# A two-block diffusion transformer on one core: the first layer's shift and scale as TensorE products in four column groups

## The chip, the cores and the metric

The kernel runs on one NeuronCore of a Trainium2 chip. The metric is the device time of one execution in microseconds (us); the reported number is the median of several executions. Lower is better. The engines that appear below are TensorE (PE in the profile; its weight loads are PEld), VectorE (DVE), ScalarE (ACT), GpSimd (POOL) and SyncE (SP), whose queue issues all loads and stores.

## The reference

256 tokens of 1024 features pass through four transformer layers, two of a first block and two of a second. Everything is float32. Each layer makes six modulation vectors of 1024 numbers from a condition vector `c`, and uses two of them, a shift and a scale, before its mixer:

```python
c_act = jax.nn.silu(c)
mod = jnp.einsum('bd,dm->bm', c_act, w_mod[i]) + b_mod[i]     # 1024 -> 6 * 1024
sh_a, sc_a, gt_a, sh_f, sc_f, gt_f = jnp.split(mod, N_MOD, axis=-1)
h = modulate(rmsnorm(x, g_mix_pre[i]), sh_a, sc_a)            # norm * (1 + scale) + shift
qkv = jnp.einsum('bsd,de->bse', h, w_qkv[i])
```

After `qkv` come a stick-breaking attention, an output projection and a gated feed-forward network; the other three layers are alike in form. All that matters here is the very beginning: layer 0 can't start its first projection before the shift and scale of its features exist, and these are 2 x 1024 dot products of length 1024 against 8.4 MB of weights.

## The kernel before, in words

**Precision.** Weights arrive in float32. Most products are made three times in a reduced format (`mm3`, line 611): each operand is split into a rounded part (`wh`, `hh`) on ACT and a remainder (`wl`, `hl`) on DVE (`split`, line 601), and the products high-high, high-low and low-high are added in PSUM.

**Loads.** Weights come as 1 MB chunks (`chunk`, line 594; 128 partitions x 2048 floats) through SP's queue. A chunk needs one of 3 buffers of class K8; a half chunk (128 x 1024 floats) needs one of 32 buffers of class K4.

**Order.** The builder records every operation in program order. A planner (`schedule`, line 382) then replays them with a cost for each operation and picks, whenever an engine is free, the ready operation that was recorded first; the result is a fixed order per engine for the whole program. At run time each engine follows its order strictly. All operations are issued from one helper, so the profile's line is always L543 and tiles have to be told apart by name.

**The first stage** (`first_values`, line 966) makes layer 0's values `v` (256 x 1024). It runs over four rounds `q`, each with two of the eight feature tiles of 128. `mods(q)` loads four half chunks of modulation weights and makes the shift and the scale for the two tiles; then the transposed, normalized tokens (`tps`) are scaled and shifted to `hf` and split to `h0h`/`h0l` (tiles 0 to 3) or `h1h`/`h1l` (4 to 7); then the round's 1 MB chunk of value weights is split and 24 products of 128 x 512 are added into the PSUM tiles `acc`. In the recorded order `mods(q + 1)` stands ahead of the 24 products of round `q`. When `acc` is complete, ACT copies it out as `v` and the query and key projections (`qkps`) begin.

In the kernel before, `mods` makes each column by a dot product on DVE: the weights are laid out transposed, so that partition p holds the 1024 weights of output feature p, and `dot` (line 673) multiplies them with `c_act`, which TensorE has spread over all partitions (`on_all_rows`, the tiles `rowps` and `rows`), and adds along the row. The bias enters as the starting value. There are 16 such dot products in the stage (2 vectors x 8 tiles); `scale_of` (line 684) then turns a scale into (1 + scale) * gain.

Of the kernel before, what the change touches and what calls it, by code (L numbers as in the profile page):

```python
# [10 lines left out]
F32 = mybir.dt.float32  # L11
# [3 lines left out]
ALU = mybir.AluOpType  # L15
AX = mybir.AxisListType
PSUM = bass.MemoryType.PSUM

P = 128
D = 1024  # L20
S = 256
KT = D // P
# [559 lines left out]
class Builder:  # L582
# [41 lines left out]
    def setup(self):  # L624

        nc, io = self.nc, self.io
        self.mhalf = self.const.tile([P, 16], F32, tag="mhalf", name="mhalf")
        nc.gpsimd.memset(self.mhalf, -0.5)
        self.cact = self.const.tile([P, 24], F32, tag="cact", name="cact")
        nc.sync.dma_start(out=self.cact, in_=self.io["vecs"][:, 0:24])  # L630
        self.eye = self.const.tile([P, P], F32, tag="eye", name="eye")
        nc.sync.dma_start(out=self.eye, in_=io["consts"][:, 0:P])
        self.vec = self.const.tile([P, NVEC], F32, tag="vec", name="vec")
        nc.sync.dma_start(out=self.vec[:, 0 : self.FIRST], in_=self.io["vecs"][:, 0 : self.FIRST])
        nc.scalar.activation(out=self.cact, in_=self.cact, func=AF.Silu)
        self.cb = {0: self.on_all_rows(self.cact[:, 0:8])}

    def setup_x(self):
# [327 lines left out]
    def first_values(self):  # L966

        nc, io = self.nc, self.io
        self.setup()
        acc = self.new_acc()  # L970
        self.h = self.new_ht("h")
        self.raw["sc_a"] = self.sb.tile([P, 8], F32, name="raw")

        def mods(q):
            for k in range(2):
                f = q * 2 + k
                i = len(self.plan)
                self.plan.append([("w_mod", 0, None, 1, a * D + f * P, D) for a in range(2)])
                for a, kind in enumerate(("sh_a", "sc_a")):
                    w = self.sb.tile([P, D], F32, name="w0")  # L980
                    nc.sync.dma_start(out=w, in_=io["wst"][i][:, a * D : (a + 1) * D])
                    if f + a == 0:
                        self.setup_x()
                    self.dot(w, self.cb[0], 0, 0, kind, f)
                self.scale_of(0, 0, "sc_a", f, 1)

        mods(0)
        xn = [self.normed(self.x[t], None, self.xe[t]) for t in range(2)]
        for q in range(4):
            w = self.w.load()  # L990
            tps = self.first_tps(xn, q)
            for k in range(2):
                kt = q * 2 + k
                a, b = self.modcols["sc_a"][:, kt : kt + 1], self.modcols["sh_a"][:, kt : kt + 1]
                h = self.sb.tile([P, 2, P], F32, name="hf")
                if k == 0:
                    nc.vector.tensor_scalar(out=h, in0=tps[:, k], scalar1=a, scalar2=b, op0=ALU.mult, op1=ALU.add)
                else:
                    nc.scalar.activation(out=h, in_=tps[:, k], func=AF.Identity, scale=a, bias=b)
                hh, hl = self.hm(self.h, kt)  # L1000
                nc.scalar.copy(hh, h)
                nc.vector.tensor_tensor(out=hl, in0=h, in1=hh.bitcast(F32), op=ALU.subtract)
            if q < 3:
                mods(q + 1)
            w = self.w.take(w)
            for t in range(2):
                for k in range(2):
                    self.acc_mm(acc, t, self.hx(self.h, t, q * 2 + k), w[k], q + k == 0, q + k == 4)
        nc.after = nc.ops[-1]
        self.setup_rest()  # L1010
        nc.after = None
        return self.evict_v(acc)
# [629 lines left out]
```

## Time and profile before

| | |
|---|---|
| median of 3 runs | 1364.46 us (1360.81 to 1364.98) |
| the profiled execution's own time | 1364.06 us |
| span of that execution's instructions | 1362.2 us |
| mean granted TensorE clock | 0.991 of full speed |
| HBM read | 309.35 MB |

All stretches below are microseconds from the start of the span. A "busy" share of PE counts the modelled length of pipelined products, so a PE that is busy 10 of 10 us may still work more slowly than it can; the spacing of the starts of its products says more. DVE, ACT and DMA shares can be read as they stand. A bracket behind a row of the timeline gives the idle time of that engine before the instruction and what ended it. A merged row (x4) gives the start of its first instruction.

### The profile page before, as it was taken

The numbers are of one execution on the slowest core, as the hardware profiler recorded it, in microseconds if no ns is written. First come the engines' busy times: TensorE is split into PE (matmuls) and PEld (weight loads), VectorE is DVE, ScalarE is ACT, GpSimd is POOL, SyncE is SP. The second block draws the span as 40 slices with busy tenths as digits, with TensorE's granted clock in tenths as the row PEclk, the third lists the DMA queues.
The fourth block names the chain that finished last, engine by engine and source line by source line (L and its number), as shares of the span: only waits on it lengthen the run. The fifth ranks groups of instructions, "written<-read, shape, count | busy, mean of one in ns | idle before, by whom it ended". The sixth has DMA issues, their size and how long they took to land.

```text
span 1362.2 us, 22161 instructions
## 1 busy us (share of the span) xinstructions
PE 1327.6 (97%) x8872; PEld 1195.2 (88%) x8872; DVE 1084.7 (80%) x1817; ACT 715.6 (53%) x1241; POOL 73.0 (5%) x102
## 2 busy tenths in 40 slices
PE   5999899999999999999999999999999999899998
PEld 4887799999888799999888888899999899899997
DVE  7888888998988599999799987876767998755542
ACT  3664665555666474546543567854444536544430
POOL 0000100000100000001023111200000000000000
PEclk8999899999999999999999999999999999999999
DMA  9856578887676156777454531587776688455520
GB/s 361 322 223 255 207 280 318 321 327 294 240 250 263 50 201 255 278 257 281 182 187 158 212 121 66 190 315 255 273 277 255 228 311 307 147 194 186 186 94 32
DMA packets 45319, 311.83 MB, mean 229 GB/s; under 512 B 5280, under 2 KB 5664, under 8 KB 8864
## 3 DMA queue, kind: packets, MB, share of 16 engines
q1 hardware_dynamic: 45216, 310.42, 61.2%
q8 instruction: 69, 1.13, 0.3%
q14 instruction: 34, 0.28, 0.1%
HBM read 309.35 MB, written 1.05 MB: 228 GB/s over the span
## 4 chain that ended last, share of the span: by engine, by line
PE 92%; DVE 4%; ACT 2%; issue 1%; DMA 0%; POOL 0%; SPq 0%; ACTq 0%; DVEq 0%
PE gu L543 34%; PE acc L543 31%; PE qkps L543 7%; PE fp L543 4%; PE cu L543 3%; PE z L543 2%; PE dz L543 2%; PE bb L543 2%; PE qps L543 2%; DVE w L543 1%; PE op L543 1%; PE dop L543 1%; PE kc L543 1%; PE tps L543 1%; PE atp L543 1%; DVE u L543 1%
## 5 line engine op out<-in xcount | busy, mean ns | idle before, releaser
L543 DVE TENSOR_TENSOR wl<-w,wh 128x1024 fp32r<-128x1024 f32 x392 | 471.3, 1221 | 77.3 <-ACT wh L543 54.3
L543 ACT CAST wh<-w 128x1024 fp32r<-128x1024 f32 x392 | 402.8, 1049 | 102.9 <-DMA w<-in_wst_dram 62.2
L543 DVE CUSTOM_DVE_ANT_0 w<-w,rows,vec 128x1024 f32<-128x1024 f32 x192 | 242.2, 1279 | 12.9 <-DMA w<-in_wst_dram 12.7
L543 PE MATMUL gu<-h1h,wh 128*128 128x256 f32 x640 | 181.4, 283 | 0.0
L543 PE MATMUL gu<-h1h,wl 128*128 128x256 f32 x640 | 181.1, 283 | 0.0
L543 PE MATMUL gu<-h0h,wl 128*128 128x256 f32 x640 | 181.1, 283 | 0.0
L543 PE MATMUL gu<-h1l,wh 128*128 128x256 f32 x640 | 181.1, 283 | 0.0
L543 PE MATMUL gu<-h0l,wh 128*128 128x256 f32 x640 | 181.1, 283 | 0.0
L543 PE MATMUL gu<-h0h,wh 128*128 128x256 f32 x640 | 181.0, 283 | 0.0
L543 PE MATMUL acc<-wh,yh 128*128 128x512 f32 x352 | 137.6, 392 | 0.0
L543 PE MATMUL acc<-wl,yh 128*128 128x512 f32 x352 | 137.5, 391 | 0.0
L543 PE MATMUL acc<-wh,yl 128*128 128x512 f32 x352 | 135.7, 389 | 0.0
L543 PEld LDWEIGHTS gu<-h0h,wh 128*128 128x128 f32 x640 | 122.5, 192 | 2.3
L543 PEld LDWEIGHTS gu<-h0l,wh 128*128 128x128 f32 x640 | 122.6, 192 | 2.2
L543 PEld LDWEIGHTS gu<-h1l,wh 128*128 128x128 f32 x640 | 122.8, 192 | 0.1
L543 PEld LDWEIGHTS gu<-h1h,wl 128*128 128x128 f32 x640 | 122.8, 192 | 0.0
L543 PEld LDWEIGHTS gu<-h1h,wh 128*128 128x128 f32 x640 | 122.8, 192 | 0.0
L543 PEld LDWEIGHTS gu<-h0h,wl 128*128 128x128 f32 x640 | 122.6, 192 | 0.1
L543 DVE TENSOR_TENSOR y<-s,gu 128x256 f32<-128x256 f32 x80 | 33.5, 418 | 77.0 <-ACT s L543 76.9
L543 ACT ACTIVATE s<-gu 128x256 f32<-128x256 f32 x40 | 15.4, 385 | 137.2 <-PE gu L543 137.2
L543 PEld LDWEIGHTS acc<-wh,yl 128*128 128x128 f32 x352 | 66.1, 188 | 14.2
L543 PEld LDWEIGHTS acc<-wh,yh 128*128 128x128 f32 x352 | 66.4, 188 | 12.3 <-ACT yh L543 0.2
(358 smaller groups left out, 2752.2 us busy)
## 6 DMA issues: line engine op xcount, KB each, us to landing
w<-in_wst_dram SPq DMA_DIRECT2D x284, 1024.0 KB, 4.9
w<-in_wst_dram SPq DMA_DIRECT2D x16, 512.0 KB, 11.4
x<-in_x_dram SPq DMA_DIRECT2D x2, 512.0 KB, 5.9
cx<-in_ctx_dram SPq DMA_DIRECT2D x2, 512.0 KB, 6.2
out_dram<-x SPq DMA_DIRECT2D x1, 512.0 KB, 2.6
out_dram<-x SPq DMA_DIRECT2D x2, 256.0 KB, 2.0
cst<-in_consts_dram SPq DMA_DIRECT2D x1, 264.0 KB, 5.2
smalls<-in_smalls_dram SPq DMA_DIRECT2D x1, 256.0 KB, 5.2
```

What stands on the lines that cost most here:

```text
L543: fn(*[real(a) for a in op.args], **{k: real(v) for k, v in op.kw.items()})
```

## The change

Layer 0's shift and scale are no longer dot products on DVE. The weights are laid out in their natural orientation: a load brings 128 rows (inputs) of four row tiles by 256 output columns. For each of the two vectors, TensorE multiplies `c_act` (one column per row tile, repeated 32 times) with these weights: 4 products run in 4 column groups of the array, each of 32 columns, and write to 32 partitions each of one PSUM tile; a second set of 4, from the second half chunk, is added. So 8 products of 128 x 32 by 128 x 256 in plain float32 make, per vector, 4 partial sums of 256 outputs, each repeated on 32 partitions. ACT copies the 128 x 512 tile to SBUF. Then 4 small products with the column `four` (one 1 in each of the four groups of 32 partitions) add the four partial sums and turn the rows into columns, and DVE adds the bias. `scale_of` runs once per round over two columns in place of twice over one.

The bytes loaded, the number and size of the loads and their place in the recorded order stay the same.

```diff
@@ setup
         nc.scalar.activation(out=self.cact, in_=self.cact, func=AF.Silu)
+        self.four = self.const.tile([P, 1], F32, tag="four", name="four")
+        nc.vector.tensor_reduce(
+            out=self.four, in_=self.eye.rearrange("p (a d) -> p a d", a=4)[:, :, 0], axis=AX.X, op=ALU.add
+        )
         self.cb = {0: self.on_all_rows(self.cact[:, 0:8])}
@@ first_values
         def mods(q):
-            for k in range(2):
-                f = q * 2 + k
-                i = len(self.plan)
-                self.plan.append([("w_mod", 0, None, 1, a * D + f * P, D) for a in range(2)])
-                for a, kind in enumerate(("sh_a", "sc_a")):
+            i = len(self.plan)
+            self.plan += [[("w_mod", 0, 0, KT, a * D + q * S, S)] for a in range(2)]
+            ps = self.pmm.tile([P, 512], F32, name="gv")
+            for a in range(2):
+                ws = []
+                for h in range(2):
                     w = self.sb.tile([P, D], F32, name="w0")
-                    nc.sync.dma_start(out=w, in_=io["wst"][i][:, a * D : (a + 1) * D])
-                    if f + a == 0:
+                    nc.sync.dma_start(out=w, in_=io["wst"][i + a][:, h * D : (h + 1) * D])
+                    ws.append(w)
+                    if q + a + h == 0:
                         self.setup_x()
-                    self.dot(w, self.cb[0], 0, 0, kind, f)
-                self.scale_of(0, 0, "sc_a", f, 1)
+                for h in range(2):
+                    for g in range(4):
+                        kt = h * 4 + g
+                        nc.tensor.matmul(
+                            ps[32 * g : 32 * g + 32, a * S : (a + 1) * S],
+                            lhsT=self.cact[:, kt : kt + 1].to_broadcast([P, 32]),
+                            rhs=ws[h][:, g * S : (g + 1) * S], start=h == 0, stop=h == 1,
+                        )
+            gv = self.sb.tile([P, 512], F32, name="gvs")
+            nc.scalar.copy(gv, ps)
+            for c in range(4):
+                nc.tensor.matmul(
+                    ps[:, c : c + 1], lhsT=gv[:, c * P : (c + 1) * P], rhs=self.four, start=True, stop=True
+                )
+            f = 2 * q
+            for a, (kind, out) in enumerate((("sh_a", self.modcols["sh_a"]), ("sc_a", self.raw["sc_a"]))):
+                nc.vector.tensor_tensor(
+                    out=out[:, f : f + 2], in0=ps[:, 2 * a : 2 * a + 2], in1=self.v(f"b00{kind}", f, 2), op=ALU.add
+                )
+            self.scale_of(0, 0, "sc_a", f, 2)
```

## Rows read from the trace of the kernel before

**Rows 1.** Two lines of the page: busy time of each engine over the whole span, and the granted TensorE clock in 40 slices of 34 us, in tenths of full speed.

```profile
PE 1327.6 (97%) x8872; PEld 1195.2 (88%) x8872; DVE 1084.7 (80%) x1817; ACT 715.6 (53%) x1241; POOL 73.0 (5%) x102
...
PEclk8999899999999999999999999999999999999999
```

**Rows 2.** The first stage cut into stretches, one row each: length, busy us (and instructions) of PE, PEld, DVE, ACT, POOL, then the granted TensorE clock, the DMA share and GB/s.

```profile
10.00:17.00 7.00, 3.74 (x16) 2.70 (x16) 6.31 (x14) 1.76 (x5) 0.61 (x1) 1.00 1.02 417
17.00:24.00 7.00, 6.29 (x15) 4.94 (x16) 6.31 (x10) 2.58 (x4) 0.00 (x0) 0.51 1.03 416
24.00:34.00 10.00, 6.53 (x28) 4.78 (x27) 10.00 (x20) 3.55 (x6) 0.00 (x0) 1.00 1.02 412
34.00:38.00 4.00, 4.00 (x12) 3.10 (x11) 4.00 (x7) 2.11 (x4) 0.00 (x0) 0.57 1.03 419
38.00:49.44 11.44, 10.43 (x46) 8.28 (x45) 10.06 (x17) 7.37 (x11) 0.00 (x0) 1.00 0.67 254
```

**Rows 3.** The chain of work that ended last, from 38 us on: start, length, what.

```profile
39.66 1.20 DVE w L543
...
40.86 1.15 DVE wl L543
42.01 0.04 issue
42.05 7.55 PE acc L543 x32
49.60 10.43 PE qkps L543 x87
```

**Rows 4.** DVE's groups of instructions in the first 49.5 us: tiles, shapes, count, then busy us and mean ns of one, then idle time before.

```profile
L543 DVE CUSTOM_DVE_ANT_0 w<-w,rows,vec 128x1024 f32<-128x1024 f32 x16 | 20.2, 1279 | 6.9 <-DMA w<-in_wst_dram 6.9
L543 DVE TENSOR_TENSOR wl<-w,wh 128x1024 fp32r<-128x1024 f32 x11 | 13.3, 1220 | 2.4 <-ACT wh L543 2.4
L543 DVE TENSOR_SCALAR hf<-tps,msc_a,msh_a 128x256 f32<-128x256 f32 x4 | 2.2, 539 | 0.0
...
L543 DVE SCALAR_TENSOR_TENSOR msc_a<-raw,vec 128x1 f32<-128x1 f32 x8 | 1.2, 153 | 0.0
```

**Rows 5.** ACT's timeline: start us, length us, instruction, idle time before and what ended it.

```profile
4.39 0.59 ACT L543 COPY rows<-rowps 128x512 f32<-128x512 f32 x1 [1.66 <-PE rowps L543]
...
23.33 1.05 ACT L543 CAST wh<-w 128x1024 fp32r<-128x1024 f32 x1 [4.42 <-DMA w<-in_wst_dram]
25.84 0.41 ACT L543 CAST h0h<-hf 128x256 fp32r<-128x256 f32 x1 [1.46 <-DVE hf L543]
...
30.93 1.05 ACT L543 CAST wh<-w 128x1024 fp32r<-128x1024 f32 x1 [2.97 <-DMA w<-in_wst_dram]
...
38.74 1.06 ACT L543 CAST wh<-w 128x1024 fp32r<-128x1024 f32 x1 [2.43 <-DMA w<-in_wst_dram]
```

**Rows 6.** PE's timeline of the first stage, same columns.

```profile
17.71 2.08 PE L543 MATMUL acc<-wh,h0h 128*128 128x512 f32 x4 [2.84 <-ACT wh L543]
...
20.01 0.63 PE L543 MATMUL acc<-wh,h0l 128*128 128x512 f32 x1
20.43 0.63 PE L543 MATMUL acc<-wl,h0h 128*128 128x512 f32 x1
...
25.33 0.50 PE L543 MATMUL acc<-wl,h0h 128*128 128x512 f32 x1 [0.84 <-DVE wl L543]
...
33.69 0.50 PE L543 MATMUL acc<-wl,h0h 128*128 128x512 f32 x1 [2.63 <-DVE wl L543]
...
42.05 0.50 PE L543 MATMUL acc<-wl,h1h 128*128 128x512 f32 x1 [1.01 <-DVE wl L543]
...
49.44 0.28 PE L543 MATMUL qkps<-h0h,wh 128*128 128x256 f32 x1
49.55 0.28 PE L543 MATMUL qkps<-h0l,wh 128*128 128x256 f32 x1
```

**Rows 7.** PE's timeline in the attention of layer 0, where float32 products run in two column groups of 64 (`op`, written as 128*64; every such product is two records, so x4 is one product in each of two groups).

```profile
118.32 0.65 PE L543 MATMUL op<-at,v 128*64 128x256 f32 x4
118.90 0.39 PE L543 MATMUL qkps<-h0h,wh 128*128 128x256 f32 x1
119.13 0.28 PE L543 MATMUL qkps<-h0l,wh 128*128 128x256 f32 x1
119.34 0.44 PE L543 MATMUL op<-at,v 128*64 128x128 f32 x4
119.70 0.50 PE L543 MATMUL acc<-wh,ol 128*128 128x512 f32 x1
120.04 0.39 PE L543 MATMUL acc<-wh,oh 128*128 128x512 f32 x1
120.27 0.39 PE L543 MATMUL acc<-wl,oh 128*128 128x512 f32 x1
```

**Rows 8.** What PE waited for between 42 and 160 us: total us, times, longest (the two largest of four).

```profile
PE tps L543 <- DVE u L543: 1.8, 1, 1.8
PE fp L543 <- ACT h0h L543: 1.2, 2, 0.7
```

## The prediction, made before the changed kernel was built or run

> **What bounds the kernel now.** I read the busy shares first, then the first stage cut into stretches, then the chain, and last the engines' timelines. Over the whole span PE is busy 97% and its granted clock is 9 tenths or more in all slices but the first [rows 1]: the kernel as a whole is bound by TensorE. The change touches only the first 49 us, so it is that stage that has to be read.
>
> There three limits lie close together. DVE: its busy time is 6.3 of 7 us, 6.3 of 7, 10 of 10 and 4 of 4 from 10 to 38 us [rows 2], and the chain runs through its dot products and remainders up to 42.01, where PE takes over [rows 3]. Of its work the 16 dot products are 20.2 us [rows 4]. DMA: its share is 1.02 or 1.03 at 412 to 419 GB/s through the same four stretches [rows 2], so it is full as well. The casts of three rounds' value weights wait for their loads and start at 23.33, 30.93 and 38.74 [rows 5]: one round (2.1 MB of modulation weights, 1 MB of value weights) takes 7.6 to 7.8 us. PE: in the stage it has real idle times, 0.84 us before 25.33, 2.63 before 33.69 and 1.01 before 42.05 [rows 6], and from 17 to 24 and from 34 to 38 its granted clock is 0.51 and 0.57 [rows 2], so mostly the lower of its two levels, 1.2 GHz, in place of 2.4. At half clock the products of 128 x 512 start 0.42 us apart (20.01, 20.43); at full clock they take 7.39 / 32 = 0.23 us each between 42.05 and 49.44 [rows 6].
>
> PE's time from its first product at 17.71 to the first query-key product at 49.44 is 31.7 us: 96 products at 0.23 are 22.1, the three idle times 4.5, and what is left, 5.1, is the half clock (by the stretches 0.49 x 6.3 + 0.43 x 4 = 4.8, which fits). So PE's slack in this stage is 9.6 us, and this is what the new products have to fit into.
>
> **What is removed.** 16 dot products of 1.28 us leave DVE, and 4 of the 8 small `msc_a` operations of 0.15 [rows 4]. That takes DVE off the path: what it keeps between two rounds, two remainders of 1.22, `hf` 0.54 and a few smaller ones, is about 4 us of a round's 7.6. Late next is DMA, and then PE.
>
> The best that this can give follows from the loads. The number, size and order of the loads stay, and DMA is full, so the last value weights still arrive at 38.7 [rows 5]. Then one cast of 1.05 and 24 products at 0.23 (5.5) follow: the stage can't end before 45.3, 4.1 us earlier than 49.44.
>
> **What is added on PE.** Each round has 16 products of 128 x 32 by 128 x 256 in float32, in four sets of four, one set for each half chunk of loads. The trace has no set of four groups, but it has the same product in two groups of 64 columns: from 118.32 to the next product's start at 118.90 is 0.58 us [rows 7]. Around it, PE loses time on changing to the divided array and back. The gap before `op` at 119.34 is 0.21 (from 119.13) where such products run 0.11 apart (49.44 to 49.55 [rows 6]); after it, 118.90 to 119.13 is 0.23 in place of 0.11, and 119.70 to 120.04 is 0.34 where the next, to 120.27, is 0.23 [rows 7]. So a set costs 0.10 + 0.58 + 0.11 = 0.79 us at full clock between other products. Of the 0.58, 256 columns stream for 0.44 (twice the 0.22 by which it is longer than the 0.36 of the `op` with 128 columns, 119.34 to 119.70). Below, if the changes fall into idle time, a set is 0.58 or nothing; above, if four groups run as two pairs, 0.44 more, and if not at all side by side, 1.3 more. I take 0.79, since two groups do run side by side here and their cost is that of one.
>
> The Trainium skill, "TensorE: Matmul & The Clock Gate", section "Measured speedup vs the span model", gives a speedup of 2.38 for three column tiles, so a bit less than the number of tiles; no row here has three or four. An estimate from that figure (3 / 2.38 = 1.26 times the 0.44 of streaming) would put 0.11 on each set, 1.2 us on the sum.
>
> The sets stand ahead of the preceding round's 24 products in the recorded order, and the loads arrive one half chunk of 0.5 MB each 1.27 us (0.524 MB at 415 GB/s [rows 2]), so I expect them one by one between these products, and count both changes for each. The four sets of round 0 fall before 17.7, where PE has little to do (3.74 busy of 7 us [rows 2]). Round 1's first load arrives near 17.0 (23.33 less 2.5 for the chunk of 1 MB and less three of 1.27), before the first product; 11 sets stay on the path: 11 x 0.79 = 8.7 us.
>
> The small products: four per round, in float32 with a full weight load of 128 columns and one column streamed, two records each as for `op`. No row has one column. A product with 128 columns of weights and 256 streamed takes 0.11, one with 512 streamed 0.23 [rows 6, 7]; the floor is nothing, the ceiling 8 x 0.23 = 1.8 per round. I take the nearer, 8 x 0.11 = 0.9; rounds 1 to 3 make 2.7 us. The Trainium skill, "TensorEngine Tiling (Array Packing)", section "Instruction Overhead", puts a matmul with one column at the same some 60 cycles as one with 60, which is 25 ns at full clock; as an estimate 0.2 per round, and the sum would be 2.1 us less by it. No run here shows it yet.
>
> **What is added elsewhere.** The copy of 128 x 512 on ACT is 0.59 (as `rows` [rows 5]); ACT is busy 1.8 to 3.6 of each stretch before 38 [rows 2], so it is hidden except in the chain from a round's last load to its first product. DVE gets two additions and one `msc_a` of some 0.15 [rows 4] per round, and the one reduction for `four` lies in the 6.9 us in which DVE waits for its first load [rows 4]. The tiles `gv` take one of the four PSUM buffers in which the transposed tokens stand early; a transpose then comes later, in PE's idle time before 17.7, and at the worst four of them (0.11 each as above) come into a chain.
>
> The chain behind a round's last set: copy 0.59, small products 0.9, additions and scale 3 x 0.15, `hf` 0.54, cast 0.41 [rows 4, 5], with hand-overs of 0.04 [rows 3] about 3.1 us. In round 0 it begins near 13.2 (the last load of the round: 17.0 less 1.27 and less 2.5) and ends near 17 to 18; before, the first product ran at 17.71: no change, give or take 0.7. In rounds 1 to 3, 2.2 us of the chain aren't PE's own. Products of the preceding round that the planner puts behind the set cover this; how many is not to be seen, so PE stands idle 0 to 2.2 us each time. I take 0.5, as PE lags behind its loads by then: 1.5 us are left of the 4.5.
>
> A PE set that waits for its load holds up all products queued behind it, up to 1.27 us for each load that comes later than the planner thought. SP's queue waits less: its chunk buffers come free when DVE has made the remainders, which is now sooner, so the query-key chunks are there earlier; nobody waits for them before PE is done with `acc`.
>
> **The clock.** PE was half idle before 17 and clocked at 0.51 from 17 to 24, and idle for 2.6 us up to 33.69 before the 0.57 from 34 to 38 [rows 2, 6]. With the sets in between, PE has no such idle time after 17. I take the second loss as gone and half of the first as left: 1.7 us of 5.1. Bounds: 0 and 5.1.
>
> **The sum.** 17.7 + 22.1 (products) + 8.7 (sets) + 2.7 (small products) + 1.5 (idle) + 1.7 (clock) = 54.4 against 49.4: PE becomes the bound, and the stage ends 5 us later although 20 us of DVE work are gone. A round costs PE 5.5 + 3.2 + 0.9 = 9.6 us at full clock and DMA 7.6.
>
> Behind the stage, PE's largest waits for other engines up to 160 us are 1.8 and 1.2 us in all [rows 8], so what is lost is not made up, and a fuller stock of split weights has nothing to feed. The planner sets a new order for the whole program; that may shift a microsecond or two either way. The profiled execution's own time is 1364.06, 0.4 below the median of the runs: 1364.1 + 5 = 1369.1. I predict 1369.
>
> **Bounds.** With every unknown at its low end (sets at 0.58, small products and idle nothing, full clock) the sum falls by 2.3 + 2.7 + 1.5 + 1.7 to 46.2, 3 us before the old end. With two pairs (+4.8), small products at 1.8 (+2.7), idle 2.2 (+5.1) and the clock as before (+3.4), it is 16 us more than my sum.
>
> **Rivals.**
> 1. *PE has room, and DMA ends the stage.* It decides at a PE round below the 7.6 us of DMA, so with sets and small products at 2.1 per round in place of 4.1. For it: the floors above, PE's 9.6 us of slack. Against: the 0.79 of rows 7, measured around the same kind of product. The end is then 45.3 to 46: 1360.5, not slower. Chance 0.19.
> 2. *Four groups don't run four wide.* As two pairs 11 x 0.44 = 4.8 more: 1374; one by one 11 x 1.3 = 14 more: 1383. For it: no row shows more than two. Against: these two start together at the cost of one. Chance 0.16.
> 3. *It doesn't matter.* What the chain on DVE gives back is what PE loses, or the new order makes up for it: 1364. For it: all three limits lie within 4 us of each other. Against: the waits of rows 8 are too small to be made up. Chance 0.07.
>
> **How the numbers follow.** My forecast has 0.58, with its own range from 1364 to 1374. A measurement of this kernel can tell about 0.3%, 4 us, from no change. Faster by more: only the better half of rival 1, 0.09. Within: the rest of rival 1 (0.10), rival 3 (0.07) and the lower half of the forecast (0.25), 0.42. Slower by more: 0.33 of the forecast and rival 2 (0.16), 0.49. The range from 1361 to 1377 leaves out the best of rival 1 and the worst of rival 2, some 0.16.
>
> **What would show it.** In the changed kernel DVE's busy share from 10 to 38 us falls to about half, DMA stays full until near 39, PE has no idle time above 1 us from 18 us to the first `qkps`, and this starts near 54. A set takes 0.58 us from its first product to the next other product and 0.1 more on either side. I am wrong if `qkps` starts before 50, if the sets are far from 0.8, or if PE is at half clock for longer than before.

## The result, and the profile after

The changed kernel takes 1372.21 us (median of 6 runs, 1368.69 to 1373.23) against 1364.86 for the kernel before in the same comparison (6 runs, 1360.81 to 1366.05). The ratio is 1.0055, with a 95% interval from 1.0038 to 1.0072: slower by 0.55%, about 7 us. The profiled execution took 1372.94 us with a span of 1371.2, so 9.0 us more span than the one before; sums against the profile are made with that.

Two lines of the changed kernel's page show where to look (busy time of each engine; granted clock in 40 slices):

```profile
PE 1343.2 (98%) x9032; PEld 1199.3 (87%) x9032; DVE 1066.7 (78%) x1790; ACT 717.2 (52%) x1245; POOL 70.3 (5%) x102
...
PEclk9999999999999999999999999999999999999999
```

DVE has lost 18.0 us of work and PE has gained 15.6 [rows 1]. The two slices of the clock that stood at 8, the first and the fifth, are now at 9. The first stage, cut at nearly the same places as before (columns as in rows 2):

```profile
10.00:17.00 7.00, 5.80 (x36) 2.82 (x36) 1.76 (x4) 1.19 (x3) 0.94 (x2) 1.00 1.03 418
17.00:24.00 7.00, 5.65 (x29) 3.13 (x33) 3.96 (x8) 3.40 (x6) 0.00 (x0) 0.68 1.02 410
24.00:34.00 10.00, 10.00 (x63) 6.01 (x56) 2.40 (x6) 3.06 (x5) 0.00 (x0) 0.88 1.02 405
34.00:38.00 4.00, 4.00 (x29) 2.10 (x27) 1.56 (x2) 0.58 (x2) 0.00 (x0) 1.00 1.05 429
38.00:50.00 12.00, 12.00 (x83) 7.11 (x81) 3.96 (x8) 5.04 (x8) 0.00 (x0) 1.00 0.42 168
```

The third number behind the length is DVE: 1.76, 3.96, 2.40 and 1.56 us from 10 to 38, where it was 6.31, 6.31, 10.00 and 4.00 [rows 2]. DMA (the number before the last) is full up to 38 and at 0.42 behind it, so the loads no longer set the pace. PE, the first number behind the length, is busy without a gap from 24 to 50. It is what remains. Its timeline (start us, length us, instruction; in brackets the idle time before it and what ended that):

```profile
10.89 1.33 PE L543 MATMUL tps<-eye,xn 128*128 128x128 f32 x5 [2.78 <-DVE xn L543]
12.15 1.08 PE L543 MATMUL gv<-w,cact 128*32 128x256 f32 x8
13.16 1.54 PE L543 MATMUL tps<-eye,xn 128*128 128x128 f32 x6
14.63 1.08 PE L543 MATMUL gv<-w,cact 128*32 128x256 f32 x8
15.65 0.48 PE L543 MATMUL tps<-eye,xn 128*128 128x128 f32 x1
16.05 0.64 PE L543 MATMUL gv<-w,cact 128*32 128x256 f32 x8
17.40 1.05 PE L543 MATMUL gv<-four,gvs 128*128 128x1 f32 x8 [0.71 <-ACT gvs L543]
18.92 0.63 PE L543 MATMUL tps<-eye,xn 128*128 128x128 f32 x4 [0.47 <-DVE raw L543]
20.04 1.22 PE L543 MATMUL acc<-wh,h0h 128*128 128x512 f32 x2 [0.49 <-ACT h0h L543]
...
26.51 0.40 PE L543 MATMUL acc<-wl,h0h 128*128 128x512 f32 x1
26.84 0.64 PE L543 MATMUL gv<-w,cact 128*32 128x256 f32 x8
27.41 0.50 PE L543 MATMUL acc<-wh,h0l 128*128 128x512 f32 x1
27.75 0.40 PE L543 MATMUL acc<-wl,h0h 128*128 128x512 f32 x1
...
30.38 0.95 PE L543 MATMUL gv<-four,gvs 128*128 128x1 f32 x8
31.18 0.47 PE L543 MATMUL acc<-wl,h0h 128*128 128x512 f32 x1
31.50 0.39 PE L543 MATMUL acc<-wh,h0l 128*128 128x512 f32 x1
...
52.28 1.20 PE L543 MATMUL acc<-wh,h1h 128*128 128x512 f32 x4 [0.55 <-ACT h1h L543]
...
57.85 0.28 PE L543 MATMUL qkps<-h0h,wh 128*128 128x256 f32 x1
```

Five things are to be seen here.

- The stage ends at 57.85 and not at 49.44 [rows 6]: 8.4 us later. Behind it the program takes 1371.2 - 57.85 = 1313.35 us, before it was 1362.2 - 49.44 = 1312.76. So 8.4 of the 9.0 us arise in the stage.
- A set (`gv<-w,cact`, x8 records are the four products) at full clock: the gap before it is 26.84 - 26.51 = 0.33 where such products run 0.23 apart, the next product follows 0.57 later, and the gap after that is 0.34. Its price is 0.57 + 0.10 + 0.10 = 0.77.
- The four small products take 31.18 - 30.38 = 0.80, and the gap behind is 0.32, so 0.9 in all.
- Ahead of 16 us PE had the lower clock: the set at 12.15 takes 13.16 - 12.15 = 1.01 where the one at 26.84 takes 0.57. The clock column of the table reads 1.00 there, so for the start of a trace the spacing of equal products is the surer sign.
- Between 20.04 and 57.85 there is one idle time, 0.55. The first products behind 20.04 run at the lower clock: 0.68 of 7 us and 0.88 of 10 in the table are (0.32 x 7 + 0.12 x 10) = 3.4 us lost, of which some 0.3 lie ahead of 20.04, so some 3.1 behind it.

From that the stage adds up: 20.04 + 96 products at 0.23 (22.1) + 12 sets at 0.77 (9.2) + 3 x 0.9 (2.7) + idle 0.55 + clock 3.1 = 57.7, against 57.85 measured.

### The profile page after: what moved, and what is told of

It reads as the page before. It is cut to its first block, busy times and chain, and to the rows that moved or that the text cites. A ratio compares the mean times of both kernels' runs of the same rounds, so it can differ in the third digit from the quotient of the medians.

```text
span 1371.2 us, 22455 instructions
## 1 busy us (share of the span) xinstructions
PE 1343.2 (98%) x9032; PEld 1199.3 (87%) x9032; DVE 1066.7 (78%) x1790; ACT 717.2 (52%) x1245; POOL 70.3 (5%) x102
## 4 chain that ended last, share of the span: by engine, by line
PE 93%; ACT 2%; DVE 2%; issue 1%; DMA 1%; POOL 0%; SPq 0%; POOLq 0%; ACTq 0%; DVEq 0%
PE gu L543 34%; PE acc L543 32%; PE qkps L543 7%; PE fp L543 4%; PE cu L543 3%; PE z L543 2%; PE dz L543 2%; PE bb L543 2%; PE qps L543 2%; PE tps L543 1%; PE op L543 1%; PE gv L543 1%; PE kc L543 1%; PE atp L543 1%; PE dop L543 1%
## 5 line engine op out<-in xcount | busy, mean ns | idle before, releaser
L543 DVE CUSTOM_DVE_ANT_0 w<-w,rows,vec 128x1024 f32<-128x1024 f32 x176 | 221.8, 1278 | 8.2 <-DMA w<-in_wst_dram 8.0
```

Source lines behind the costliest of these rows:

```text
L543: fn(*[real(a) for a in op.args], **{k: real(v) for k, v in op.kw.items()})
```

## The experiments

Theory: PE bounds the stage; sets and small products (9.2 + 2.7 = 11.9 us) stand where idle time (4.5) and half clock (5.1) were, and the start is later by 2.3. Rivals: the four column groups don't run side by side; DVE's time was worth something and is given back elsewhere; the chain from a round's last load to its first product is the bound. All ratios are to the kernel before on the same chip; "end" is the first query-key product in the profiled execution. First products, ends and spans are of one execution each, the medians of all. One stretch at the lower clock costs 1.7 us in e9 below, so a difference of that size between two ends need not come from the edit.

| kernel | median us | ratio [95%] | first `acc` | end | span |
|---|---|---|---|---|---|
| the change | 1372.21 | 1.0055 [1.0038, 1.0072] | 20.04 | 57.85 | 1371.2 |
| e4: dots on DVE as well | 1369.2 | 1.0039 [1.0026, 1.0052] | 19.25 | 56.92 | 1367.2 |
| e3: two column groups | 1374.02 | 1.0066 [1.0044, 1.0087] | 22.68 | 63.50 | 1373.2 |
| e6: transposes later | 1368.74 | 1.0030 [1.0017, 1.0043] | 17.76 | 52.86 | 1365.9 |
| e1: half the sets | 1372.9 | 1.0063 [1.0047, 1.0079] | 19.54 | 57.18 | 1370.8 |
| e8: e6, half the sets, same order | 1365.16 | 1.0002 [0.9992, 1.0011] | 18.72 | 50.59 | 1364.5 |
| e2: e6, sets in one block | 1369.11 | 1.0031 [1.0019, 1.0043] | 21.56 | (mixed) | 1365.6 |
| e5: scale back on DVE | 1367.42 | 1.0024 [1.0014, 1.0034] | 18.95 | 52.26 | 1364.3 |
| e7: e5 with e6 | 1367.0 | 1.0013 [1.0003, 1.0022] | 19.04 | 53.56 | 1366.6 |
| e9: e7, value weights first | 1365.57 | 1.0019 [1.0004, 1.0033] | 18.00 | 53.36 | 1363.8 |
| e10: e6, value weights first | 1370.32 | 1.0035 [1.0021, 1.0049] | 19.99 | 56.41 | 1368.8 |

### e4: is DVE's relief worth anything?

Two unused dot products are put back on DVE behind each set pair, 16 in all:

```diff
+                for h in range(2):
+                    jk = self.sb.tile([P, D], BF16, name="djunk")
+                    nc.vector.tensor_tensor_reduce(
+                        out=jk, in0=ws[h], in1=self.cb[0], scale=1.0, scalar=self.v("b00sh_a", 0),
+                        op0=ALU.mult, op1=ALU.add, accum_out=self.extra[:, h : h + 1],
+                    )
```

> The changed kernel with 16 dot products of the old size put back on DVE, on the same half chunks, their results unused. Theory (PE is the bound, DVE's relief is worth nothing by itself): DVE's 20 us more hide beside PE, only a dot product that stands ahead of an addition or hf in a chain shows; the first query-key product 0 to 2 us later than 57.85. Rival (DVE's relief has made up for part of the loss, as DVE was the path before): 4 us or more later.

The stage ends at 56.92, 0.9 earlier than with the change alone, where 0 to 2 later had been expected: the planner's order is another one, and the first product comes 0.8 earlier. From the first product to the end the two take the same, 56.92 - 19.25 = 37.7 and 57.85 - 20.04 = 37.8. DVE's busy time is back (third number, windows as above):

```profile
30.00:40.00 10.00, 10.00 (x68) 6.16 (x68) 8.93 (x18) 4.63 (x7) 0.00 (x0) 1.00 0.78 316
```

So the time that DVE was given is worth nothing once PE carries the sets; DVE could do both. The whole is 3.0 us shorter than the change by the medians (the intervals overlap), and that isn't from the stage: behind it the program takes 1367.2 - 56.92 = 1310.3 against 1313.35, in another order that the planner made, and with a granted clock of 0.94 in place of 0.89 from 150 to 180 us, which is 1.5 us of it.

### e3: do the four groups run side by side?

Two column groups of 64 in two passes, in place of four of 32:

```diff
-                    for g in range(4):
-                        kt = h * 4 + g
+                    for j in range(2):
+                        for g in range(2):
+                            r = j * 2 + g
+                            kt = h * 4 + r
```

> The same products in two column groups of 64 in place of four of 32, so a set of four is two pairs, one after the other, and each streams 256 columns twice. Theory (four groups run side by side, and a set's price is 0.44 of streaming and 0.33 of changing over): 12 sets of the three later rounds cost 0.44 more each at full clock, 5.3 us, and those at half clock somewhat more; the first query-key product at 63 to 65.5, the time 5 to 8 us above the changed kernel. Rival (a set's price is the change of the array's division, streaming is hidden): within 1 us of the changed kernel.

The timeline of PE in e3:

```profile
28.57 0.40 PE L543 MATMUL acc<-wl,h0h 128*128 128x512 f32 x1
28.89 1.08 PE L543 MATMUL gv<-w,cact 128*64 128x256 f32 x8
29.91 0.50 PE L543 MATMUL acc<-wh,h0l 128*128 128x512 f32 x1
30.25 0.40 PE L543 MATMUL acc<-wh,h0h 128*128 128x512 f32 x1
```

The same 8 records now take 29.91 - 28.89 = 1.02 in place of 0.57: 0.45 more, one further pass of 256 columns. So the set with four groups did run four wide. The stage ends 5.65 later, 2.6 of it ahead of the first product. Behind that it is 3.0 more and not the 5.3 expected: the planner put five of the twelve sets in two blocks (two from 36.63, three from 47.59), which saves changes of the array, and the idle time of 0.55 is gone. The whole rose by less, 1.8 us by the medians where 5 to 8 had been expected, as the rest took 1373.2 - 63.50 = 1309.7.

### e6: why is the first product late?

The transposes of rounds 1 to 3 are allowed only after round 0's shift and scale:

```diff
         mods(0)
+        mark = nc.ops[-1]
...
+            nc.after = mark if q else None
             tps = self.first_tps(xn, q)
+            nc.after = None
```

> The changed kernel with the transposes of rounds 1 to 3 ordered behind round 0's shift and scale, so that the sets of round 0 don't stand behind 12 transposes at the lower clock. In the changed kernel the first product of the values starts at 20.04, 2.3 us later than before. Theory (that late start comes from the transposes ahead of the sets of round 0 and is paid at the end of the stage): first product at 18 to 19, first query-key product 1 to 2 us earlier than 57.85. Rival (the loads and the chain behind them set it): within 0.5 us.

PE's timeline of e6:

```profile
12.86 1.54 PE L543 MATMUL gv<-w,cact 128*32 128x256 f32 x16
15.12 1.05 PE L543 MATMUL gv<-four,gvs 128*128 128x1 f32 x8 [0.71 <-ACT gvs L543]
...
17.76 0.73 PE L543 MATMUL acc<-wh,h0h 128*128 128x512 f32 x2 [0.22 <-ACT h0h L543]
...
20.45 0.73 PE L543 MATMUL acc<-wh,h0l 128*128 128x512 f32 x2
21.02 0.63 PE L543 MATMUL acc<-wh,h0h 128*128 128x512 f32 x2
21.48 0.39 PE L543 MATMUL acc<-wl,h0h 128*128 128x512 f32 x1
```

Here the last two sets of round 0 run one after the other from 12.86, so their loads were there; in the change they stood at 14.63 and 16.05, with seven transposes ahead of and between them, where e6 has two (two more of its four stand ahead of the second set, where the change has five). The first product comes at 17.76, 2.3 earlier. The stage ends 5.0 earlier: a gain of 1 to 2 had been expected. 2.3 are the start, and nearly all of the rest is the clock. The products are 0.23 apart from the start (21.48 - 21.02 is 0.46 for two), so the half clock is gone in this execution. The one wait behind the first product is 0.5, for `h1h`. The sum without the clock is 17.76 + 22.1 + 9.2 + 2.7 + 0.5 = 52.3, measured 52.86: the terms hold at full clock. Why the higher clock was granted here is not shown; e7 and e10, with the same edit, came to their first products later and e7 ran these at the lower one.

### e1 and e8: what do the sets cost?

e1 makes only the first of each vector's two sets, so half of each sum is left out:

```diff
-                for h in range(2):
+                for h in range(1):
```

> Leaves out half of the sum over inputs: only the first half chunk of each vector is multiplied, so 2 sets of four products per round in place of 4; all loads, copies and small products stay. In the changed kernel the first query-key product starts at 57.85 us and the median time is 1372.2. Theory (the sets lie on PE's path, 0.77 us each at full clock with the changes of the array's division): 6 of 12 sets gone are 4.6 us, and the two sets gone before the first product some 1 to 2 more; the first query-key product starts at 51 to 53.5, the time is 1366 to 1368. Rival (the late start of the first product and the new order are the cause, the sets fit into idle time): the start of the query-key products moves by less than 2 us.

A miss: the end hardly moved. ACT's timeline and then PE's of e1 show why:

```profile
26.96 0.59 ACT L543 COPY gvs<-gv 128x512 f32<-128x512 f32 x1 [6.22 <-PE gv L543]
30.18 0.41 ACT L543 CAST h0h<-hf 128x256 fp32r<-128x256 f32 x1 [2.63 <-DVE hf L543]
30.49 0.56 ACT L543 ACTIVATE hf<-tps,msh_a,msc_a 128x256 f32<-128x256 f32 x1
30.95 1.03 ACT L543 CAST wh<-w 128x1024 fp32r<-128x1024 f32 x1
```

```profile
30.13 0.40 PE L543 MATMUL acc<-wh,h0l 128*128 128x512 f32 x1
32.03 0.50 PE L543 MATMUL acc<-wh,h0h 128*128 128x512 f32 x1 [1.50 <-ACT wh L543]
```

The planner made another order, in which ACT casts the round's value weights (`wh`, 30.95) behind the copy, `h0h` and `hf` of the chain. PE then waits 1.50, 1.50 and 1.27 in rounds 1 to 3. So the round stays as long as with all sets (the copies on ACT are at 26.96 and 36.68, 9.7 apart), bound now by the chain and the casts behind it. In this order they are as long as PE's work was with all sets; whether they were so in the changed kernel's own order, e1 can't say. To tell the price from the order, e8 takes e6 with its order as it is and drops the second set of each vector only when the instructions are written out (half of each sum is left out; its helper's line is L548):

```diff
-                    fn(*[real(a) for a in op.args], **{k: real(v) for k, v in op.kw.items()})
+                    kw = {k: real(v) for k, v in op.kw.items()}
+                    if op.fn == "matmul" and op.kw["lhsT"].shape[1] == 32:
+                        if not op.kw["start"]:
+                            continue
+                        kw["stop"] = True
+                    fn(*[real(a) for a in op.args], **kw)
```

> The kernel with late transposes (e6_late_tps), planned as it is, but the second set of each vector is left out when the program is written, so every engine keeps its order and half of the sum over inputs is missing. There the first product starts at 17.76 and the first query-key product at 52.86. Theory (in a fixed order a set costs PE 0.77 us in rounds 1 to 3): 6 sets less are 4.6 us, less what shows as new waits; the first query-key product at 48 to 49.5. Rival (the chain from a round's last set to its first product bounds the round, as the waits of e1_half_sets suggest): 51 or later, with waits of more than 1 us per round on PE.

The end is at 50.59, between the theory's 49.5 and the rival's 51. From the first product to the end it takes 50.59 - 18.72 = 31.9 against 35.1 in e6, 3.2 less where six sets at 0.77 are 4.6. One wait is new (total us, times, longest; the 0.5 was there in e6):

```profile
PE acc L548 <- ACT h1h L548: 0.5, 1, 0.5
PE acc L548 <- DVE wl L548: 0.2, 1, 0.2
```

Its first two products also ran at the lower clock, 1.13 us for two up to the next set in place of 0.66 in e6: 0.5 more. With these two, 3.9 of the 4.6 are found; 0.7 is not accounted for. (The lower clock is also why the first product comes 1.0 later than in e6, with two sets fewer ahead of it: its 12 transposes and 4 small products take 18.72 - 14.54 = 4.2 us, in e6 17.76 - 15.12 = 2.6.) The whole is as long as before the change (1.0002). So the sets cost most of their price when nothing else moves, and with the later transposes half the sets is about where the change would break even.

### e2: can the switching be saved?

e6 with the four sets of a round behind each other, after the round's last load:

```diff
+            wss = []
             for a in range(2):
...
+                wss.append(ws)
+            nc.after = last
+            for a in range(2):
+                ws = wss[a]
...
+            nc.after = None
```

> Late transposes, and in addition the four sets of a round stand in one block (all wait for the round's last load in the planned order). Theory (a set's price is 0.44 of streaming and 0.33 of changing the array's division there and back): one change per round in place of four, 3 x 3 x 0.2 to 0.33 = 2 to 3 us less on PE, of which waits for the round's last load give some back: the first query-key product at 50 to 52 against 52.86. Rival (changes cost nothing that isn't hidden): 52.5 or later.

PE's timeline of e2:

```profile
12.55 3.64 PE L543 MATMUL gv<-w,cact 128*32 128x256 f32 x32
...
21.56 0.50 PE L543 MATMUL acc<-wh,h0h 128*128 128x512 f32 x1 [2.24 <-ACT h0h L543]
...
23.15 1.93 PE L543 MATMUL gv<-w,cact 128*32 128x256 f32 x32
25.01 0.50 PE L543 MATMUL acc<-wh,h0h 128*128 128x512 f32 x1
```

A block of four sets takes 25.01 - 23.15 = 1.86 at full clock and two switches, about 2.1 against 4 x 0.77 = 3.1: 1 us a round is to be saved, as expected. But the first block starts at 12.55 at the lower clock and lasts 3.64, the chain begins behind all of it, and the first product comes at 21.56, 3.8 later than in e6. The one pays for the other: 1369.11 and 1368.74. (Some query-key products were placed among the last value products, so the end mark can't be compared.)

### e5, e7, e9, e10: half the work on each engine

e5 makes the shift on PE and the scale by dot products on DVE, so that neither has all:

```diff
+            for k in range(2):
+                self.dot(ws[2 + k], self.cb[0], 0, 0, "sc_a", f + k)
```

> Half of the change: the shift is made by products on PE (two sets per round), the scale by the old dot products on DVE (two per round); the loads are the same. Theory (three limits lie close together, DVE before, PE after): PE's round is 5.5 + 2 x 0.77 + 0.5 = 7.5 us, DVE's about 7, DMA's 7.6, so no engine is over DMA; the first query-key product at 48 to 51, the later end if PE has the lower clock for 7 us again; the time 1361 to 1365. Rival (the chain of hand-overs over PE and ACT bounds a round as soon as the products are on PE): 54 or later.

e7 is e5 with e6's later transposes:

> The split of e5_split with the late transposes of e6_late_tps. Theory: the first product at 17 to 18, the full clock from then on, and no engine over DMA's 7.6 us per round: the first query-key product at 46 to 48.5, 1 to 3 us ahead of the kernel before (49.44), the time 1361 to 1364 against 1364.3. Rival (the chain of hand-overs bounds a round): 50 or later, no faster than before.

Both missed: the stage ends at 52.26 and 53.56. The rounds are 8.6 us (ACT's copies of e5 at 32.18 and 40.78), between DMA's 7.6 and the 9.6 that the whole change costs PE. Waits of e7's PE from 17 to 57:

```profile
PE acc L543 <- ACT wh L543: 3.9, 4, 1.5
```

In e5 and e7 PE waits in each round for a cast of value weights, which stands on ACT behind the chain as in e1. e9 tests whether that place is the cause: it is e7 with each round's value weights loaded, and so cast, ahead of the round's modulation weights. e10 does the same to e6.

```diff
+        nxt = self.w.load()
         for q in range(4):
-            w = self.w.load()
+            w = nxt
...
             if q < 3:
+                nxt = self.w.load()
                 mods(q + 1)
```

> As e7 (shift on TensorE, scale by dot products on VectorE, later transposes), but each round's value weights are loaded ahead of that round's modulation weights, so that their casts stand ahead of the copy of the row products in ACT's order. If the 0.8 us that PE waited in each round of e7 for a cast of value weights came from the cast's place behind the chain on ACT, the waits on `wh` fall below 0.2 each, and the first query-key product comes at 49 to 52 us, the whole at 1362 to 1366. If the chain from a round's last load to its first product is the limit in itself, the same idle time comes back under another name (`gvs`, `h0h`, `h1h`), the first query-key product stays at 52 to 54, and the whole stays within 2 us of e7.

> As e6 (shift and scale both on TensorE, later transposes), with each round's value weights loaded ahead of its modulation weights. If PE's own work bounds the stage (sets and small products 11.9 us beside 22.1 of value products), nothing is to be had: the first query-key product at 52 to 53.5 as in e6. If waits for the chain were hidden in e6 by products of the round before, these are fewer behind the last sets now, and each of rounds 1 to 3 shows 0.5 to 2 us of idle time on `gvs`, `h0h` or `h1h`: 54 to 57.

Waits of e9's PE:

```profile
PE acc L543 <- ACT h0h L543: 2.2, 1, 2.2
PE acc L543 <- ACT wh L543: 1.5, 1, 1.5
PE acc L543 <- ACT h1h L543: 0.5, 1, 0.5
```

Its one wait on `wh` is the one ahead of the first product; behind it there are none, so the cast's place was where PE waited. But 2.2 on `h0h` and 0.5 on `h1h` came in its stead, 2.6 us in all where e7 had 3 x 0.8 = 2.4, and the end stayed at 53.36: the idle time came back under another name, as the second reading had it. Not all of the end is the chain, though. The waits stand in rounds 1 and 2 only, and from 30 to 40 the granted clock is 0.83 in e9, 1.7 us lost that e7 doesn't lose there.

Nor is all of the chain needed. DVE's timeline of e9, round 1:

```profile
27.67 0.16 DVE L543 TENSOR_TENSOR msh_a<-gv,vec 128x2 f32<-128x2 f32 x1 [3.52 <-PE gv L543]
27.75 1.28 DVE L543 CUSTOM_DVE_ANT_0 w<-w,rows,vec 128x1024 f32<-128x1024 f32 x1
29.28 0.54 DVE L543 TENSOR_SCALAR hf<-tps,msc_a,msh_a 128x256 f32<-128x256 f32 x1
```

DVE stands idle for 3.52 until the small products are done, adds the bias to the shift, and only then makes the round's second dot product, whose half chunk had landed at 23.51. So 1.28 us of the chain in e9 come from DVE's fixed order and not from anything that the dot product waits for. It is the same in e5 and e7 (in e7 the addition at 26.37 waits 3.45, the dot product starts at 26.45). A kernel with this dot product ahead of the addition wasn't run; whether it would beat the one before is open.

In e10 the end is 56.41, inside the second reading's 54 to 57 but not for its reason. PE stands idle for 1.1 in place of e6's 0.5, in round 1 alone (0.7 of it for `gvs`), where each of three rounds was to show 0.5 to 2. The larger parts are the clock: from 30 to 40 it is 0.83, 1.7 us lost, and the first product is 2.2 later than in e6 because the same sets, small products and transposes ahead of it, in the same order, began 0.3 later and ran longer at the lower clock (the 12 transposes and what follows up to the first product take 19.99 - 17.54 = 2.45 us, in e6 17.76 - 16.03 = 1.73, and the small products ahead of them 1.73 and 0.91). So e10 doesn't show that products of the round before had covered the chain.

None of these kernels beats the one before. e8 comes level with half the sum left out; of the complete ones e7 and e9 come nearest, with intervals that begin just above 1.

## Why the prediction was right, and where it was off

The direction and the mechanism were right: PE becomes the bound, the stage ends later although 20 us of DVE work are gone. 1369.0 was forecast, 1372.21 came, inside the range, which was wide: a chance of 0.49 stood on slower by more than 4 us. The stage lost 8.4 us where 5 were forecast. Term by term:

| term | predicted | measured |
|---|---|---|
| first product | 17.7 | 20.04 |
| 96 products | 22.1 | 22.1 |
| sets | 11 x 0.79 = 8.7 | 12 x 0.77 = 9.2 |
| small products | 3 x 0.9 = 2.7 | 3 x 0.9 = 2.7 |
| idle | 1.5 | 0.55 |
| half clock | 1.7 | 3.1 |
| end of the stage | 54.4 | 57.85 (sum 57.7) |
| rest of the program | 0, "a microsecond or two either way" | +0.6 |

- **The price of a set** was taken from two column groups in the attention [rows 7] and held to 0.02. That four groups run at the cost of one, rival 2's question, is shown by e3. An estimate from the Trainium skill, "TensorE: Matmul & The Clock Gate", section "Measured speedup vs the span model", had 0.11 more on each set for three column tiles; the trace has nothing of that with four (0.57 from the set's first product to the next, where two groups took 0.58 [rows 7]).
- **The small products** are the 0.9 read off rows 6 and 7. The Trainium skill, "TensorEngine Tiling (Array Packing)", section "Instruction Overhead", gave 0.2 per round by 60 cycles for one column; the 8 records take 0.80, 0.10 each, so the page's 60 cycles don't hold for this form. Each of its records has a full weight load of 128 columns, which may be why; no run here varies that.
- **The step that failed most** is the start: "in round 0 it begins near 13.2 ... and ends near 17 to 18 ...: no change, give or take 0.7". The chain itself was 20.04 - 16.6 = 3.4 where 3.1 was put. What failed is its beginning: the last set of round 0 ran at 16.05, though in e6, from the same loads, it starts near 13.7 (the second half of the 16 records from 12.86). PE takes its instructions in a fixed order, and 12 transposes stood ahead of that set where e6 has only round 0's 4; the 8 of later rounds took some 0.2 to 0.25 us each at the lower clock (13.16 to 14.63 for six). I had the transposes down as work in idle time. e6 shows it: with them moved, the first product is at 17.76, where the prediction had it.
- **The clock** was under-estimated: 3.1 of the old 5.1 stayed, not 1.7. The second loss, from 34 to 38 [rows 2], did go. In e6 the first went too. It depends on more than the place of the sets, and I didn't find on what. From 17 us on PE was not at half clock for longer than before: a clock of 0.68 over 7 us and 0.88 over 10 is half clock for 4.5 + 2.4 = 6.9 us, and 0.51 over 7 and 0.57 over 4 [rows 2] for 6.9 + 3.4 = 10.3. So this sign of being wrong didn't come.
- **A misread row:** the granted clock stands at 8 tenths in the fifth slice too, not only in the first [rows 1]. No term of the sum rests on it, but it bears on the rest of the program, below.
- **Sets on the path** were twelve, as the late start put all of round 1 behind it (0.5 more, with the lower price of one). **Idle time** was less by 1.0, which pays for that.
- **DMA and DVE** behaved as forecast: DMA was full up to 38, DVE's share fell to below half. Rival 1 (DMA ends the stage) needed a PE round below 7.6; it was 9.6 to 9.75 (the small products of rounds 1 to 3 start at 30.38, 40.13 and 49.73).
- **The room on PE**, put as 9.6 us of slack, was the right quantity but not all of it could be filled: idle and clock fell from 9.6 to 3.65, so 5.95 of the 11.9 us of new work were absorbed. The other 5.95 and the 2.3 at the start make 8.3 of the 8.4.

What stays open is the rest of the program. Across these kernels it takes from 1309.7 (e3) to 1313.9 us (e8). One wait in it changes from kernel to kernel (PE waits for `u`, columns as above; the changed kernel from 57 to 160 us):

```profile
PE tps L543 <- DVE u L543: 3.3, 1, 3.3
```

It is 1.8 before [rows 8], 1.3 in e4 and absent in e3, as the planner lays the whole program out anew. But it is 3.3 in e6 too, and 1.8 in e9, so it doesn't explain the spread. The clock goes with it better: from 150 to 180 us the granted clock is 1.00 in e9 and 0.94 in e3 and e4, whose rest takes 1309.7 to 1310.4; it is 0.89 before the change, in the change, e1, e7, e8 and e10 and 0.83 in e6, whose rest takes 1312.4 to 1313.9 (e5 lies between, 0.94 and 1312.0). From 1.00 to 0.89 of 30 us is 3.3 us. What sets the clock there is not shown. These few us are no property of the change that a run here shows, yet they are as large as what the stage gains in e7 or e9 over the change.

## What to carry to other kernels

Work that is moved off a busy engine has to be priced on the engine that takes it, between its neighbours there, with the switch into and out of the divided array: here 20 us of DVE work became 11.9 us on PE, and PE had just half of that free. Where three limits lie within a few us of each other, relieving one shows the next (PE's work, then the chain of hand-overs and the orders on ACT and DVE in it), and none of the edits tried here got past them all. With a fixed order per engine, ask of each moved instruction what it now stands behind: the first product came 2.3 us late, most of it behind transposes that nobody needed yet, and in e9 a dot product whose weights were there waited 4 us behind an addition.

## What the runs showed of the hardware that was not expected

Four column groups of float32 products with 256 columns take no longer than two (0.57 and 0.58); changing to the divided array and back costs about 0.10 on either side, and sets that follow one another pay it once (a block of four takes 1.86 to the next product, where four single sets take 4 x 0.57 = 2.28 and eight such changes). A product that streams a single column isn't nearly free: 0.10 for each of its two records, next to 0.11 for a product that streams 256 and 0.23 for one that streams 512 [rows 6]. And a stretch with the lower clock came and went with a change of order far smaller than the work in it: e6 ran its first stage at the higher clock from its first value product on, e7 with the same edit ran products 0.43 apart after 20 us (22.22 and 22.65). Three times the lower clock came with or right behind an idle time of PE: 2.63 us before the change [rows 6], 2.2 in e9, 0.7 and 0.4 in e10; but the 1.50 that PE waited in round 1 of e1 brought none (granted clock 1.00 from 30 to 40).
